# An encoder's attention, by pairs of heads and halves of the queries

## The chip, the cores and the metric

One core of a Trainium2 chip runs the whole kernel as one program. The metric is the device time of one execution in microseconds; lower is better. Engine names are those of the profile: PE is TensorE, PEld its weight loads, DVE VectorE, ACT ScalarE, POOL GpSimd, SP the queue that issues most DMAs.

## The reference

Two encoder layers over 1024 tokens of width 1024, in float32. The even layer mixes tokens by latent attention (8 heads, q and k of 96 features, v of 64) and by retention, the odd layer by gated linear attention; each ends in a gated MLP. The change touches the attention alone:

```python
q = _rmsnorm(q, q_head_norm); k = _rmsnorm(k, k_head_norm)      # then rotary on the last 32 features
def block(qi):
    s = jnp.einsum('bqhd,bkhd->bhqk', qi, k).astype(jnp.float32) * MLA_QK ** -0.5
    p = jax.nn.softmax(s, axis=-1).astype(v.dtype)
    return jnp.einsum('bhqk,bkhe->bqhe', p, v)
```

## The kernel before

Most products are made in float32 precision from two parts: an operand is cast to float32r on ACT (`hi`) and the rest is taken on DVE or POOL (`lo = x - hi`, `split`, L327 to L330). `mm3` (L348 to L354) then makes three matmuls, hi by hi, hi by lo and lo by hi. A matmul of two plain float32 operands does it in one call, which stands in the trace as two records.

The attention is written in class `Mla`. `produce(pr)` makes q, k and v of a pair of heads for all tokens (plain float32 matmuls, L1555 and L1557), with v split, and with 64 columns of ones beside v (zeros in the low part). `prepare(i)` transposes q and k of a head, splits them, and finds each query's largest score over keys with 16 matmuls of 128x512 (L1610), each reduced on DVE (L1611); the negated maximum becomes row 96 of q (L1619), against a row of ones in k, so that the score comes out shifted. `attend(i)` goes, for one head, over two halves of 512 queries and eight tiles of 128 keys: an `mm3` for the scores, Exp on ACT (L1639), a split of the result (ACT, then DVE or every second time POOL, L1640), and, four tiles later (`AHEAD`), `product` (L1649): an `mm3` with [v, ones], so that rows 64 to 127 of the output are the softmax's denominators. After the last key tile it copies numerator and denominator (L1657, L1658); after the second head of a pair it divides (Ln, Exp, a Newton step, L1664 to L1668) and sends the result to DRAM or, for the last pair's first half, splits it.

The work is emitted by generators that are woven: `even` (L643) runs, for each head i, `attend(i)` with 16 steps and beside it `prepare(i + 1)` (13 steps) and, for even i below 6, `produce` of the next pair (10 steps); with heads 6 and 7 it runs the first operands and weights of the output projection (`early`, `weights`). A scheduler in the tile framework can move instructions from that order where they are ready. PSUM has eight banks: five of one rotation (`mm`), three of the other (`mr`, for `prepare` and `produce`). SBUF tiles come from rotations by tag: `raw` 2, `w` 6, `hx` 32, `hf` 22, `hr` 16, `pg` 3 buffers.

Of the kernel before, what the change touches and what calls it, by code (L numbers as in the profile page):

```python
# [10 lines left out]
F32 = mybir.dt.float32  # L11
# [21 lines left out]
RG = 8, 17  # L33
SECOND = 5
AHEAD = 4
GLA_STEPS, GLA_TICKS = 38, (42, 34)
GATES = 6, 7, 0, 1, 2, 3, 4, 5
EARLY = 4
# [30 lines left out]
class Encoder:  # L69
# [573 lines left out]
    def even(self, h, win, ws):  # L643
# [44 lines left out]
        def many(*gens):  # L688
            for g in gens:
                yield from g  # L690
# [38 lines left out]
        def weights():  # L729
            first.append(self.out_weights(w, 0))  # L730
            yield
# [1 line left out]
        rest = many(mixed(proj_qk(3), norms()), rg(0, 1, 2, 3))  # L733
        self.weave(ret(2), 19, islice(rest, W2), W2)
        self.weave(ret(3), 19, rest, 39 - W2)
        for i in range(8):
            side, n = [], 0
            if i < 7:
                side.append(self.on((1, 1), m.prepare(i + 1)))
                n += 13  # L740
            if i % 2 == 0 and i < 6:
                side.append(self.on((0, 1), m.produce(i // 2 + 1)))
                n += 10
            if i >= 6:
                side.append(self.on((1, 0), many(early(0, 4, 5, 6, 7, 0, 1)) if i == 6 else
                                    many(early(0, 2), weights(), early(1, 4, 5, 6, 7, 0, 1, 2))))
                n += 6 if i == 6 else 9
            self.weave(m.attend(i), 2 * NT - 2 * (i < 6), many(*side), n)
        outs = [(o_a[p], None) for p in range(4)] + [(o_r[p], gates[p]) for p in range(4)]
        return outs, *o, w, [], first[0]  # L750

# [771 lines left out]
class Mla:  # L1523


    def __init__(self, e, outs, parts):
        self.e, self.nc, self.outs, self.parts = e, e.nc, outs, parts
        self.wq = e.io["mla_w_uq"][0].rearrange("(k p) f -> p k f", p=P)
        self.wkv = e.io["mla_w_ukv"][0].rearrange("(k p) f -> p k f", p=P)
        self.pair, self.head, self.behind = {}, {}, []  # L1530

    def produce(self, pr):

        e, nc = self.e, self.nc
        krr, krs = e.kr
        w1, w2 = (e.page(s, F32, "w") for s in ([P, 3, 192], [P, 2, 256]))
        nc.sync.dma_start(out=w1, in_=self.wq[:, :, blk(pr, 192)])
        nc.sync.dma_start(out=w2, in_=self.wkv[:, :, blk(pr, 256)])
        qp, kp, vp = [], [], []
        self.pair[pr] = qp, kp, vp  # L1540
        heads = lambda ap, f: ap.rearrange("p (n f) -> p n f", f=f)
        c2, s2 = e.rot[0]
        for hf in range(2):
            st, y, z = (e.small([P, 4, 4]) for _ in range(3))
            for t in range(4 * hf, 4 * hf + 4):
                c = t % 2
                if not c:
                    qp.append(e.page([P, 2, 192], tag="hx"))
                    kp.append(e.page([P, 2, 192], tag="hx"))
                    vp.append([e.page([P, 2, 2, P], F32R, tag="hx") for _ in range(2)])  # L1550
                    for v, x in zip(vp[-1], (1.0, 0.0)):
                        nc.gpsimd.memset(v[:, :, :, 64:].bitcast(F32), x)
                ps = e.bank()
                for k in range(3):
                    nc.tensor.matmul(ps[:, :192], lhsT=e.cq[k][hf][:, blk(t % 4)], rhs=w1[:, k], start=k == 0, stop=k == 2)  # L1555
                for k in range(2):
                    nc.tensor.matmul(ps[:, 256:], lhsT=e.ckv[k][hf][:, blk(t % 4)], rhs=w2[:, k], start=k == 0, stop=k == 1)  # L1557
                pk = heads(ps[:, 256:], 128)
                for j in range(2):
                    junk = e.half([P, P])  # L1560
                    nc.scalar.activation(junk[:, :96], ps[:, blk(j, 96)], AF.Square, accum_out=st[:, t % 4, j:j + 1])
                    nc.scalar.activation(junk[:, :64], pk[:, j, :64], AF.Square, accum_out=st[:, t % 4, 2 + j:3 + j])
                e.split(pk[:, :, 64:], *(v[:, c, :, :64] for v in vp[-1]))
                nc.vector.tensor_copy(qp[-1][:, c], ps[:, :192])
                nc.vector.tensor_copy(heads(kp[-1][:, c], 96)[:, :, :64], pk[:, :, :64])
                yield
            nc.vector.tensor_tensor(st[:, :, 2:], st[:, :, 2:], krs[:, blk(hf, 4)].unsqueeze(2).broadcast_to([P, 4, 2]), ALU.add)
            nc.vector.tensor_scalar(st, st, 1.0 / 96, EPS, ALU.mult, ALU.add)
            e.rsqrt(st, y, z)
            for i in range(2 * hf, 2 * hf + 2):  # L1570
                ts = blk(i, 2)
                q4, k4 = (x[i].rearrange("p c (n f) -> p c n f", f=96) for x in (qp, kp))
                yv = lambda o, w: y[:, blk(i % 2, 2), o:o + 2].unsqueeze(3).broadcast_to([P, 2, 2, w])
                tb = lambda v, w: v[:, ts, w].unsqueeze(2).broadcast_to([P, 2, 2, w.stop - w.start])
                nc.vector.tensor_tensor(q4, q4, yv(0, 96), ALU.mult)
                nc.vector.tensor_tensor(k4[:, :, :, :64], k4[:, :, :, :64], yv(2, 64), ALU.mult)
                nc.vector.tensor_tensor(k4[:, :, :, 64:], tb(krr, slice(0, 32)), yv(2, 32), ALU.mult)
                r = q4[:, :, :, 64:]
                a, b = e.half([P, 2, 2, 32]), e.half([P, 2, 2, 32])
                nc.vector.tensor_tensor(a, r, tb(c2, slice(0, 32)), ALU.mult)  # L1580
                for j in range(2):
                    nc.vector.tensor_tensor(b[:, :, :, blk(j, 16)], r[:, :, :, blk(1 - j, 16)], tb(s2, blk(j, 16)), ALU.mult)
                nc.vector.tensor_tensor(r, a, b, ALU.add)
            yield

    def prepare(self, i):
# [1 line left out]
        e, nc = self.e, self.nc  # L1588
        qp, kp, _ = self.pair[i // 2]
        hc = blk(i % 2, 96)  # L1590
        qs, ks = e.new_split(1), e.new_split(1)
        for t in qs.hi[0] + qs.lo[0] + ks.hi[0] + ks.lo[0]:
            nc.gpsimd.memset(t[96:].bitcast(F32), 0.0)
        for hf in range(2):
# [25 lines left out]
        self.head[i] = qs, ks  # L1620
        yield

    def attend(self, i):

        e, nc = self.e, self.nc
        qs, ks = self.head.pop(i)
        for hf in range(2):
            q, pa = qs.half(0, hf), e.bank()
            for kt in range(NT):
                if i > 5:  # L1630
                    x = e.page([P, H2], tag="hf")
                else:
                    if kt % 2 == 0:
                        two = e.page([P, 2, H2], tag="raw")
                    x = two[:, kt % 2]
                ps = e.bank()
                both = e.page([P, 2, H2], F32R, "w")
                e.mm3(ps, ks.tok(0, kt), q, True, True)
                nc.scalar.activation(x, ps, AF.Exp, scale=96 ** -0.5)  # L1639
                e.split(x, both[:, 0], both[:, 1], nc.gpsimd if kt % 2 and i < 7 else None)  # L1640
                self.behind.append((i, hf, kt, pa, both))
                if len(self.behind) > AHEAD:
                    self.product(*self.behind.pop(0))
                yield
        while self.behind and i == 7:
            self.product(*self.behind.pop(0))
            yield

    def product(self, i, hf, kt, pa, both):  # L1649
        e, nc = self.e, self.nc  # L1650
        pr, rows, cs = i // 2, blk(i % 2, 64), halves()[hf]
        e.mm3(pa, [v[:, kt % 2, i % 2] for v in self.pair[pr][2][kt // 2]], (both[:, 0], both[:, 1]), kt == 0, kt == NT - 1)
        if kt < NT - 1:
            return
        if i % 2 == 0 and not hf:
            self.o, self.den = (e.page([P, S]) for _ in range(2))
        nc.scalar.copy(self.o[rows, cs], pa[:64])  # L1657
        nc.vector.tensor_copy(self.den[rows, cs], pa[64:])  # L1658
        if i % 2:

            if not hf:
                self.y, self.outs[pr] = e.page([P, S]), e.waiting()
            o, z, y = self.o[:, cs], self.den[:, cs], self.y[:, cs]
            nc.scalar.activation(y, z, AF.Ln)  # L1664
            nc.scalar.activation(y, y, AF.Exp, scale=-1.0)
            nc.vector.scalar_tensor_tensor(z, z, -1.0, y, ALU.mult, ALU.mult)
            nc.vector.scalar_tensor_tensor(y, z, 2.0, y, ALU.add, ALU.mult)
            nc.vector.tensor_tensor(o, o, y, ALU.mult)  # L1668
            if pr == 3 and not hf:
                self.parts[pr] = hi, lo = [e.page([P, H2], F32R, "hx") for _ in range(2)]  # L1670
                e.split(o, hi, lo)
            else:
                nc.sync.dma_start(out=self.outs[pr][hf], in_=o)


def encoder(tc, io):
# [39 lines left out]
```

## Time and profile before

| | |
|---|---|
| median of 3 runs | 2552.49 us (2551.14 to 2555.01) |
| profiled execution, its time | 2551.83 us |
| profiled execution, its span | 2549.8 us |
| TensorE's granted clock, mean | 0.995 |
| PE busy | 2496.8 us (98%) |
| DVE, ACT, POOL busy | 71%, 47%, 11% |

The span reaches from the first to the last instruction; the time has 2.0 us more around it. A busy PE counts a matmul from its start to its modelled end, while the next one has already started, so that a stretch can be 98% busy without being full; the distance between starts tells more.

### The profile page before, as it was taken

Reading aid. Unit: us, or ns where it says so; the run is one execution under the profiler, and the core shown is the slowest. Engines: PE = TensorE matmul, PEld = TensorE weight load, DVE = VectorE, ACT = ScalarE, POOL = GpSimd, SP = SyncE. Lnnn points to the kernel's source line nnn. Section 1 sums busy time; section 2 is a strip of 40 time slices with the busy share of each in tenths; the row PEclk is TensorE's granted clock in tenths of the full one; section 3 lists DMA queues with packets and bytes.
Section 4 is the critical chain, followed back from the end, with each engine's and each line's share of the span. In section 5 each row is a group of like instructions: output and inputs, shape, how many; then the busy total and the mean of one; then the engine's idle time right before and its main releaser. Section 6 shows DMA issues by size and latency. Waiting matters only on the chain.

```text
span 2549.8 us, 33347 instructions
## 1 busy us (share of the span) xinstructions
PE 2496.8 (98%) x12584; PEld 2091.4 (82%) x12584; DVE 1800.3 (71%) x2855; ACT 1209.2 (47%) x2229; POOL 269.8 (11%) x286
## 2 busy tenths in 40 slices
PE   8999989999999999999999999999999999999999
PEld 8989877777888888887788898897788888887787
DVE  6545887878578877778767545648578777778762
ACT  5333767778444333334434445657444333334432
POOL 0000033443000000003240000000000000004240
PEclk9999999999999999999999999999999999999999
DMA  6111100003632333437524211223822332437523
GB/s 196 40 46 42 51 26 5 14 18 124 202 95 87 103 109 98 130 97 259 162 68 149 60 55 42 73 69 108 260 83 95 105 111 87 132 102 253 165 69 122
DMA packets 305814, 262.21 MB, mean 103 GB/s; under 512 B 15916, under 2 KB 240277, under 8 KB 305653
## 3 DMA queue, kind: packets, MB, share of 16 engines
q1 hardware_dynamic: 301045, 251.69, 31.2%
q10 hardware_dynamic: 4608, 8.39, 0.9%
q8 instruction: 99, 1.62, 0.3%
q14 instruction: 62, 0.51, 0.1%
HBM read 189.52 MB, written 70.52 MB: 102 GB/s over the span
## 4 chain that ended last, share of the span: by engine, by line
PE 68%; DVE 17%; ACT 6%; DMA 6%; issue 3%; POOL 1%; SPq 0%; DVEq 0%; ACTq 0%; POOLq 0%
PE mm L351 58%; DMA raw<-in_ffn_w_up 3%; DVE pg L1291 2%; ACT w L329 2%; DVE w L330 1%; DVE hx L1261 1%; PE mr L1104 1%; PE mr L351 1%; PE mr L1555 1%; DVE pg L1295 1%; PE mr L1557 1%; DVE hx L330 1%; DVE sr L1611 1%; DVE wf L330 1%; PE mr L854 1%
## 5 line engine op out<-in xcount | busy, mean ns | idle before, releaser
L351 PE MATMUL mm<-hx,w 128*128 128x512 f32 (+1 forms) x3408 | 831.1, 394 | 6.9 <-ACT h L329 4.9
L351 PEld LDWEIGHTS mm<-hx,w 128*128 128x128 f32 (+1 forms) x3408 | 636.3, 188 | 144.8 <-ACT w L329 5.7
L351 PE MATMUL mm<-h,w 128*128 128x512 f32 x1800 | 433.6, 394 | 7.5 <-ACT w L329 4.9
L329 ACT CAST w<-raw 128x1024 fp32r<-128x1024 f32 (+3 forms) x307 | 245.1, 802 | 347.2 <-PE mm L351 211.8
L351 PEld LDWEIGHTS mm<-h,w 128*128 128x128 f32 x1800 | 339.8, 190 | 80.5 <-ACT w L329 5.8
L330 DVE TENSOR_TENSOR w<-raw,w 128x1024 fp32r<-128x1024 f32 (+3 forms) x257 | 254.5, 993 | 177.1 <-ACT w L329 161.2
L351 PE MATMUL mm<-w,hx 128*128 128x256 f32 (+1 forms) x2304 | 363.9, 305 | 2.8 <-POOL w L330 2.3
L351 PE MATMUL mm<-h,wf 128*128 128x512 f32 x1368 | 329.2, 389 | 1.4 <-DVE wf L330 0.8
L351 PEld LDWEIGHTS mm<-w,hx 128*128 128x128 f32 x2304 | 307.4, 191 | 21.9 <-POOL w L330 3.3
L351 PEld LDWEIGHTS mm<-h,wf 128*128 128x128 f32 x1368 | 256.5, 188 | 56.3 <-DVE wf L330 1.7
L1397 POOL TENSOR_TENSOR hx<-raw 128x512 f32<-128x512 f32 (+1 forms) x10 | 12.6, 1260 | 1535.4 <-DMA raw<-in_ffn_w_down 1008.1
L329 ACT CAST wf<-raw 128x1024 fp32r<-128x1024 f32 x78 | 82.1, 1052 | 182.7 <-DVE raw L1247 134.5
L1261 DVE TENSOR_TENSOR hx<-mm,hx 128x512 f32<-128x512 f32 x190 | 130.1, 685 | 45.9 <-PE mm L351 45.9
L351 PE MATMUL mm<-hx,wf 128*128 128x512 f32 x552 | 132.1, 389 | 0.0
L351 PEld LDWEIGHTS mm<-hx,wf 128*128 128x128 f32 x552 | 103.5, 188 | 21.9 <-DVE hx L1261 0.4
L330 DVE TENSOR_TENSOR wf<-raw,wf 128x1024 fp32r<-128x1024 f32 x78 | 95.5, 1224 | 18.9 <-ACT wf L329 18.9
L351 PE MATMUL mm<-hr,hr 128*128 128x512 f32 x336 | 104.2, 404 | 1.3 <-ACT hf L1639 1.3
L1292 ACT ACTIVATE pg<-pg 128x1024 f32<-128x1024 f32 x44 | 46.7, 1062 | 121.9 <-DVE pg L1291 121.8
L1291 DVE SCALAR_TENSOR_TENSOR pg<-mm,c,pg 128x512 f32<-128x512 f32 (+1 forms) x100 | 73.7, 747 | 30.0 <-ACT pg L1286 30.0
L351 PE MATMUL mm<-hf,w 128*128 128x512 f32 x384 | 88.8, 392 | 0.0
L351 PEld LDWEIGHTS mm<-hf,w 128*128 128x128 f32 x384 | 72.2, 188 | 16.0
L330 POOL TENSOR_TENSOR w<-raw,w 128x512 fp32r<-128x512 f32 (+1 forms) x50 | 68.5, 1369 | 138.9 <-ACT w L329 96.9
(385 smaller groups left out, 3384.2 us busy)
## 6 DMA issues: line engine op xcount, KB each, us to landing
raw<-in_ffn_w_up SPq DMA_DIRECT2D x88, 512.0 KB
pg<-d SPq DMA_DIRECT2D x52, 512.0 KB
d<-tt SPq DMA_DIRECT2D x64, 256.0 KB
d<-pg SPq DMA_DIRECT2D x55, 256.0 KB
raw<-in_ffn_w_down SPq DMA_DIRECT2D x32, 384.0 KB
raw<-in_w_in_odd SPq DMA_DIRECT2D x24, 512.0 KB
raw<-in_w_out_even SPq DMA_DIRECT2D x16, 512.0 KB
rb<-in_ffn_w_down SPq DMA_DIRECT2D x32, 256.0 KB
```

Of the source, the lines that this page charges most:

```text
L329: self.nc.scalar.copy(hi, src)
L330: return (rest or self.nc.vector).tensor_tensor(lo, src, hi.bitcast(F32), ALU.subtract)
L351: mm = lambda w, x, start, stop: self.nc.tensor.matmul(out, lhsT=w, rhs=x, start=start, stop=stop, skip_group_check=more)
L854: self.nc.tensor.transpose(ps[:, blk(j)], src[:, j], self.ident)
L1104: nc.tensor.matmul(ps, lhsT=w[:, blk(t % 4)], rhs=x, start=n == 0, stop=n == len(terms) - 1)
L1261: add = lambda out, x, y: nc.vector.tensor_tensor(out, x, y, ALU.add)
L1291: nc.vector.scalar_tensor_tensor(dst, g[hf][:, src], cw(tap), dst, ALU.mult, ALU.add)
L1292: nc.scalar.activation(cv, cv, AF.Silu)
L1295: nc.vector.tensor_tensor(cv[:, sl], cv[:, sl], v[hf], ALU.mult)
L1555: nc.tensor.matmul(ps[:, :192], lhsT=e.cq[k][hf][:, blk(t % 4)], rhs=w1[:, k], start=k == 0, stop=k == 2)
L1557: nc.tensor.matmul(ps[:, 256:], lhsT=e.ckv[k][hf][:, blk(t % 4)], rhs=w2[:, k], start=k == 0, stop=k == 1)
L1611: nc.vector.tensor_reduce(mx[:, 2 * t + hf:2 * t + hf + 1], ps, AX.X, ALU.max)
```

## The change

Attention goes by pairs of heads. For each half of the queries the first head's eight key tiles are scored and exponentiated, all eight results being kept, then the second head's. The weights are not split any more: both heads' products with v are plain float32 matmuls with 64 columns of weights, the one head's into PSUM rows 0 to 63 and the other's into rows 64 to 127 of the same bank, two key tiles (four calls) at a time. The ones beside v are gone: GpSimd adds the eight exponentiated tiles of each head (seven adds of 128x512), and two plain float32 matmuls of ones with these sums make the denominators of both heads. The division follows a step later. v is not split. The generators beside it are one list, dealt out at `PACE`: 13/8 items a step for the first eight steps, then 9/8.

```diff
+PACE = 13 / 8, 9 / 8
...
-        for i in range(8):
-            side, n = [], 0
...
-            self.weave(m.attend(i), 2 * NT - 2 * (i < 6), many(*side), n)
+        order = [("p", 1)] + [x for p in range(1, 4) for x in (("k", p), ("p", 2 * p), ("p", 2 * p + 1))]
+        side = many(*(self.on((0, 1), m.produce(x)) if kind == "k" else self.on((1, 1), m.prepare(x)) for kind, x in order),
+                    self.on((1, 0), many(early(0, 4, 5, 6, 7, 0, 1, 2), early(1, 4, 5, 6, 7, 0, 1, 2), weights())))
+        done = 0
+        for i, _ in enumerate(many(*(m.attend(p) for p in range(4))), 1):
+            while done < PACE[0] * min(i, 8) + PACE[1] * max(i - 8, 0):
+                done += 1
+                next(side, None)
...
-        w1, w2 = (e.page(s, F32, "w") for s in ([P, 3, 192], [P, 2, 256]))
-        nc.sync.dma_start(out=w1, in_=self.wq[:, :, blk(pr, 192)])
+        w1, w2 = [e.page([P, 192], tag="hx") for _ in range(3)], e.page([P, 2, 256], tag="hx")
+        for k in range(3):
+            nc.sync.dma_start(out=w1[k], in_=self.wq[:, k, blk(pr, 192)])
...
-                    vp.append([e.page([P, 2, 2, P], F32R, tag="hx") for _ in range(2)])
-                    for v, x in zip(vp[-1], (1.0, 0.0)):
-                        nc.gpsimd.memset(v[:, :, :, 64:].bitcast(F32), x)
+                if t % 4 == 0:
+                    vp.append(e.page([P, 4, 2, 64], tag="hx"))
...
-                e.split(pk[:, :, 64:], *(v[:, c, :, :64] for v in vp[-1]))
+                nc.scalar.copy(vp[-1][:, t % 4], pk[:, :, 64:])
...
-        qs, ks = e.new_split(1), e.new_split(1)
+        qs, ks = (e.new_split(1, "hx" if i % 2 else None) for _ in range(2))
...
+    def attend(self, pr):
         e, nc = self.e, self.nc
         for hf in range(2):
+            acc, xs = e.page([P, 2, H2]), [[], []]
+            for j in range(2):
+                qs, ks = self.head[2 * pr + j]
+                for kt in range(NT):
+                    if j and pr == 3:
+                        x = e.page([P, H2], tag="hf")
+                    else:
+                        if kt % 2 == 0:
+                            two = e.page([P, 2, H2], tag="raw" if j else "w")
+                        x = two[:, kt % 2]
+                    xs[j].append(x)
+                    ps = e.bank()
+                    e.mm3(ps, ks.tok(0, kt), qs.half(0, hf), True, True)
+                    nc.scalar.activation(x, ps, AF.Exp, scale=96 ** -0.5)
+                    if kt:
+                        nc.gpsimd.tensor_tensor(acc[:, j], acc[:, j] if kt > 1 else xs[j][0], x, ALU.add)
+                    if j:
+                        self.behind.append((pr, hf, kt, xs[0][kt], x, acc))
+                    if self.behind and (kt % 2 if j else True) and len(self.behind) > (AHEAD - 1) * j:
+                        self.products()
+                    elif self.later and not j:
+                        self.later.pop(0)()
+                    yield
...
+    def products(self):
...
+        for pr, hf, kt, *xs, acc in [self.behind.pop(0) for _ in range(2)]:
+            if not kt:
+                self.pa = e.bank()
+            v = self.pair[pr][2][kt // 4]
+            for j in range(2):
+                nc.tensor.matmul(self.pa[blk(j, 64)], lhsT=v[:, kt % 4, j], rhs=xs[j], start=kt == 0, stop=kt == NT - 1)
+        if kt == NT - 1:
+            oy = e.page([P, 2, H2])
+            nc.scalar.copy(oy[:, 0], self.pa)
+            self.later.append(lambda: self.divide(pr, hf, acc, oy[:, 0], oy[:, 1]))
+
+    def divide(self, pr, hf, acc, o, y):
...
+        z, ps = e.half(), e.bank()
+        for j in range(2):
+            nc.tensor.matmul(ps[blk(j, 64)], lhsT=e.ones[:, :64].bitcast(F32), rhs=acc[:, j], start=True, stop=True)
+        nc.scalar.activation(y, ps, AF.Ln)
+        nc.scalar.activation(y, y, AF.Exp, scale=-1.0)
+        nc.vector.scalar_tensor_tensor(z, ps, -1.0, y, ALU.mult, ALU.mult)
+        nc.vector.scalar_tensor_tensor(y, z, 2.0, y, ALU.add, ALU.mult)
+        nc.vector.tensor_tensor(o, o, y, ALU.mult)
```

## Rows read from the trace of the kernel before

**Rows 1.** The page: span, and busy us (share) xinstructions of each engine.

```profile
span 2549.8 us, 33347 instructions
...
PE 2496.8 (98%) x12584; PEld 2091.4 (82%) x12584; DVE 1800.3 (71%) x2855; ACT 1209.2 (47%) x2229; POOL 269.8 (11%) x286
```

**Rows 2.** Busy time in stretches: the attention, then heads 2 and 3.

```profile
core 0: us, PE busy (x) PEld busy (x) DVE busy (x) ACT busy (x) POOL busy (x), PEclk, DMA share, GB/s
366.00:651.00 285.00, 273.83 (x1300) 222.59 (x1299) 234.43 (x464) 228.42 (x583) 109.66 (x138) 0.99 0.15 46
...
441.00:484.00 43.00, 42.27 (x213) 35.90 (x211) 32.17 (x76) 33.91 (x117) 15.63 (x24) 1.00 0.09 26
484.00:516.00 32.00, 29.94 (x142) 23.39 (x141) 28.56 (x53) 25.03 (x47) 16.50 (x20) 1.00 0.00 1
```

**Rows 3.** Groups by form, 366 to 651 us: busy us, mean ns | idle before.

```profile
L351 PE MATMUL mm<-w,hx 128*128 128x512 f32 x384 | 117.9, 399 | 0.5 <-POOL w L330 0.4
L351 PE MATMUL mm<-hr,hr 128*128 128x512 f32 x336 | 104.2, 404 | 1.3 <-ACT hf L1639 1.3
...
L1611 DVE TENSOR_REDUCE sr<-mr 128x1 f32<-128x512 f32 x112 | 71.3, 680 | 1.9 <-PE mr L1610 1.6
L330 POOL TENSOR_TENSOR w<-raw,w 128x512 fp32r<-128x512 f32 x48 | 63.7, 1327 | 124.5 <-ACT w L329 82.4 <-issue 14.4 <-PE mm L351 12.9
...
L329 ACT CAST w<-raw 128x512 fp32r<-128x512 f32 x96 | 59.5, 625 | 5.4 <-PE mm L351 3.1
L1639 ACT ACTIVATE raw<-mm 128x512 f32<-128x512 f32 x96 | 57.2, 604 | 26.5 <-PE mm L351 21.7 <-POOL w L330 2.0 <-issue 1.2
L1610 PE MATMUL mr<-hr,hr 128*128 128x512 f32 x112 | 43.3, 402 | 1.9 <-DVE sr L1611 1.8
L330 DVE TENSOR_TENSOR w<-raw,w 128x512 fp32r<-128x512 f32 x48 | 36.9, 769 | 11.4 <-ACT w L329 11.4
L1555 PE MATMUL mr<-w,hf 128*128 128x192 f32 x144 | 27.5, 327 | 0.0
L1557 PE MATMUL mr<-w,hf 128*128 128x256 f32 x96 | 24.6, 379 | 0.0
...
L1593 POOL MEMSET hr<- 32x512 f32 x48 | 23.4, 522 | 7.8 <-POOL w L330 2.6 <-issue 2.4 <-PE mm L351 1.9
...
L351 PE MATMUL mm<-hf,hf 128*128 128x512 f32 x48 | 14.6, 397 | 0.8 <-ACT hf L1619 0.8
```

**Rows 4.** PE in order of time: start us, us from first start to last end.

```profile
410.05 0.86 PE L351 MATMUL mm<-w,hx 128*128 128x512 f32 x3
410.75 0.86 PE L351 MATMUL mm<-hr,hr 128*128 128x512 f32 x3
```

**Rows 5.** The same view, two tokens' tiles of plain float32 matmuls in `produce`.

```profile
403.61 1.14 PE L1555 MATMUL mr<-w,hf 128*128 128x192 f32 x6
...
404.58 1.03 PE L1557 MATMUL mr<-w,hf 128*128 128x256 f32 x4
```

**Rows 6.** The same view, retention's matmuls with 64 weight columns, both heads.

```profile
196.03 0.52 PE L351 MATMUL mm<-w,hx 128*128 128x256 f32 x3
196.47 0.44 PE L835 MATMUL mr<-hr,hf 128*64 128x128 f32 x4
...
198.12 0.41 PE L837 MATMUL mr<-hr,hr 128*64 128x128 f32 x4
198.46 0.51 PE L351 MATMUL mm<-w,hx 128*128 128x256 f32 x2
```

**Rows 7.** PE's waits, 366 to 651 us: total, times, longest.

```profile
PE mr L1598 <- DVE hx L1583: 6.5, 3, 2.7
```

**Rows 8.** Busy time in stretches of 2 us about head 1's start.

```profile
414.00:416.00 2.00, 0.00 (x0) 0.00 (x0) 2.00 (x5) 1.15 (x3) 1.09 (x1) 0.96 0.00 0
416.00:418.00 2.00, 1.87 (x8) 1.65 (x9) 2.00 (x8) 0.00 (x0) 0.00 (x0) 0.50 0.00 0
```

More of the change, by code (lines that the diff above doesn't have):

```diff
@@ L735, in even @@
         self.weave(ret(3), 19, rest, 39 - W2)
-        for i in range(8):
-            side, n = [], 0
[L738 to L747, printed above, removed]
-            self.weave(m.attend(i), 2 * NT - 2 * (i < 6), many(*side), n)
+        order = [("p", 1)] + [x for p in range(1, 4) for x in (("k", p), ("p", 2 * p), ("p", 2 * p + 1))]
[6 more added lines that the diff above has]
+                next(side, None)
+        for _ in side:
+            pass
         outs = [(o_a[p], None) for p in range(4)] + [(o_r[p], gates[p]) for p in range(4)]
@@ L1529, in __init__ @@
         self.wkv = e.io["mla_w_ukv"][0].rearrange("(k p) f -> p k f", p=P)
-        self.pair, self.head, self.behind = {}, {}, []
+        self.pair, self.head, self.behind, self.later = {}, {}, [], []
     def produce(self, pr):
@@ L1549, in produce @@
                     kp.append(e.page([P, 2, 192], tag="hx"))
-                    vp.append([e.page([P, 2, 2, P], F32R, tag="hx") for _ in range(2)])
-                    for v, x in zip(vp[-1], (1.0, 0.0)):
-                        nc.gpsimd.memset(v[:, :, :, 64:].bitcast(F32), x)
+                if t % 4 == 0:
+                    vp.append(e.page([P, 4, 2, 64], tag="hx"))
                 ps = e.bank()
                 for k in range(3):
-                    nc.tensor.matmul(ps[:, :192], lhsT=e.cq[k][hf][:, blk(t % 4)], rhs=w1[:, k], start=k == 0, stop=k == 2)
+                    nc.tensor.matmul(ps[:, :192], lhsT=e.cq[k][hf][:, blk(t % 4)], rhs=w1[k], start=k == 0, stop=k == 2)
                 for k in range(2):
@@ L1621, in prepare @@
         yield
-    def attend(self, i):
+    def attend(self, pr):
         e, nc = self.e, self.nc
-        qs, ks = self.head.pop(i)
         for hf in range(2):
[L1628 to L1646, printed above, removed]
+            acc, xs = e.page([P, 2, H2]), [[], []]
[21 more added lines that the diff above has]
+                    yield
+        del self.head[2 * pr], self.head[2 * pr + 1]
+        while pr == 3 and self.behind:
+            self.products()
@@ L1647, in attend @@
             yield
-    def product(self, i, hf, kt, pa, both):
+        if pr == 3:
+            self.later.pop(0)()
+            yield
+    def products(self):
         e, nc = self.e, self.nc
[L1651 to L1673, printed above, removed]
@@ new lines, in divide @@
+    def divide(self, pr, hf, acc, o, y):
+        e, nc = self.e, self.nc
+        z, ps = e.half(), e.bank()
[6 more added lines that the diff above has]
+        nc.vector.tensor_tensor(o, o, y, ALU.mult)
+        if not hf:
+            self.outs[pr] = e.waiting()
+        if pr == 3 and not hf:
+            self.parts[pr] = hi, lo = [e.page([P, H2], F32R, "hx") for _ in range(2)]
+            e.split(o, hi, lo)
+        else:
+            nc.sync.dma_start(out=self.outs[pr][hf], in_=o)
```

## The prediction

> **What bounds the kernel now.** I read the page first: PE is busy nearly all the time and the other engines are not [rows 1], so an edit is worth what it takes from PE's own stream or from PE's waits. Busy says little here, because a matmul of 512 columns stands with 399 ns [rows 3] while three of them start within 0.70 us of each other, 0.233 us apart [rows 4]. So I count the attention by distances. In its 285 us [rows 2] PE has 384 records of products with v, 384 of scores and 112 for the maxima [rows 3]: 880 x 0.233 = 205.0 us. `produce` adds 144 records of 192 columns and 96 of 256 [rows 3]. Their distances follow from [rows 5]: (1.14 - 0.327) / 5 = 0.163 us and (1.03 - 0.379) / 3 = 0.217 us, together 44.3 us. Both are 0.85 ns a column. The other 1300 - 880 - 240 = 180 records [rows 2] are mostly of 128 columns, 0.109 us each, 19.6 us. That makes 269 us of stream and **16 us of idle PE**. Head 2, which has `produce` beside it, is full: 112 x 0.233 + 48 x 0.163 + 32 x 0.217 + 21 x 0.109 = 43.2 of its 43 us. Head 3, without, has 29.4 of 32. The idle is where DVE is late: the chain into the transposes [rows 7], once a stretch with PE empty and DVE full, after which the granted clock was 0.50, the 1.2 GHz level [rows 8].
>
> **The change part by part.**
>
> *Products with v.* Removed: 384 x 0.233 = 89.5 us. Added: 32 blocks of four plain float32 calls. A call is two records; at 0.85 ns a column one of 512 columns takes 0.434 us, so a block in series is 8 x 0.434 = 3.47 us, and more than the 12 x 0.233 = 2.80 us that it replaces. All hangs on whether the two heads' calls, with 64 weight columns each and different PSUM rows, run side by side. No attention row shows it; retention has the same arrangement at 128 columns [rows 6]: 32 records that would take 3.47 us in series are over 1.99 us after the first start, when the next full matmul starts. That is half of the series, 1.74 us, and 0.25 us for entering, leaving and imperfect pairing. I take it over: 1.74 + 0.25 = 1.99 us a block, 63.7 us in all. Bounds: 55.7 us (nothing lost at the ends) and 119 us (series, with the same 0.25).
>
> *Denominators.* Eight times two calls of ones: 0.87 + 0.25 = 1.12 us, 9.0 us (7.0 to 15.9). Before they came free with the products. So PE's stream changes by 63.7 + 9.0 - 89.5 = **-16.8 us**, between -26.8 and +45.4.
>
> The Trainium skill has a rule against this: "TensorEngine Tiling (Array Packing)", section Key Properties, says that going from one tiling mode to another drains the engine. The trace agrees that the ends cost something, but 0.25 us for both ends together, less than one matmul's length; a full drain at each end is priced among the rivals.
>
> *Splits of the weights.* ACT's 128 casts of 0.63 us (96 of them in one group, 59.5 us [rows 3]) go, and DVE's and POOL's subtractions with them. DVE's 72 at 0.7 to 0.77 us take some 53 us. These are not PE's work; they were cover for nothing, and where DVE was late they help. ACT keeps the Exp of 0.60 us a step.
>
> *GpSimd's sums.* 112 adds. The nearest row is its subtraction of the same size, 1.327 us [rows 3]: 149 us instead of 75, with some 30 us of memsets [rows 3], 179 of 270 us. It stays hidden behind PE. Queued behind an add are the next adds and `prepare`'s memsets, for which its matmuls wait; the two `raw` buffers wait for adds too, but four tiles later. Below the row I see no reason for less than 1.2 us, above it 1.4; neither matters until an add takes (270 - 30) / 112 = 2.1 us.
>
> *v unsplit, weights of `produce` in other buffers, three DMAs for one on SP.* Nothing on PE. SP has some 50 issues in the whole attention, so two more a pair are covered; without that cover, two issues of about 0.4 us at a time when the weights are needed nine steps later.
>
> *The order.* This moves idle, not work. A step of the first head (scores only) now has 0.70 us of PE besides the side work, a step of the second head 0.70 + 1.0. The maxima are where DVE is slower: an item is two matmuls, 0.47 us, and two reductions, 1.36 us [rows 3]. By the items dealt out, a pair's eight steps of maxima for its second head fall just on the first head's steps of the next stretch, and `prepare` ends in the very step before its use. Then:
> - pair 0, first eight steps (all 13 items): PE 5.6 + 3.7 + 2.3 = 11.6; DVE 16 x 0.68 and four splits of 0.7 = 13.7 and some 2 us of end chain (reduction, ACT's copy of the row): 4 us idle;
> - pairs 1 to 3, first eight: PE 1.99 + 1.12 + 5.6 + 3.7 + 0.5 = 12.9; DVE 10.9 + 2.1 for the division, and the same 2 us of chain: 2 us each, 6;
> - second half's first eight with the end of `produce`: the chain into the transposes, up to 2.7 us a time [rows 7], three times: 8;
> - the last pair's second half: ACT 8 x 0.60 + 8 x 0.62 + 1.2 = 11 against PE 1.99 + 1.12 + 5.6 = 8.7: 2.3.
>
> Together 20.4 us against 15.8 today: **+4.6 us**. Low bound 0 (the scheduler fills the holes; then -15.8), high bound twice the sum (+25), since chains can add up.
>
> **Sum.** 2551.8 (the profiled execution, 0.7 below the median shown) - 16.8 + 4.6 = 2539.6, about **2540 us**, 12 us or 0.5% less.
>
> **The rivals.**
> 1. *The holes are filled.* Heads 0, 2 and 4 run full today although DVE works there too, and with 53 us less DVE the 2 us chains may hide. Idle no more than 6 and ends at 0.1: 2551.8 - 22 - 10 = 2520. Against it: a first-head step has little PE work to draw on.
> 2. *A block slips by a record*, since a call's second record must wait for its first: +0.434 x 40 = 17.4, 2557: no change to speak of. [Rows 6] show pairs of four records throughout, which speaks against it.
> 3. *Full drain.* If each end of 40 blocks empties the array for a matmul's 0.399 us, the ends take 32 us and not 10: 2562. The rows bear out little of it. This is the rule of "TensorEngine Tiling (Array Packing)" taken at its word.
> 4. *Slower: the light stretches starve PE.* Eight stretches of first-head steps, each 3 us worse than above: a stall of 1.7 and then a clock at 0.50 as in [rows 8], which loses 1.3. 2539.6 + 24 = 2564. It decides from 12.2 / 8 = 1.5 us a stretch on. For it: DVE, POOL (9.3 of adds and 5 of memsets in eight steps) and PE are all within a few us of each other there.
> 5. *Not side by side at 512 columns*: two streams of 512 float32 columns might not be fed at once. +45.4 for -16.8: 2602. Only the width speaks for it.
>
> **How the numbers follow.** Forecast (2530 to 2547) 0.50; rival 1 (2518 to 2530) 0.18; rival 2 0.11; rival 3 0.05; rival 4 0.10; rival 5 0.05; the rest 0.01. Less than 0.2%, 5.1 us, can't be told from no change here. Faster: the first two, 0.68. Same: most of rival 2 and small shares of the forecast's neighbours, 0.12. Slower: 0.20. The range 2522 to 2558 holds the forecast, most of rival 1 and rival 2, some 0.78 to 0.8.
>
> **What would show it.** Right: records of 128x512 with 64 weight columns, eight in about 1.9 us from the block's start to the next full matmul; PE's stream in the attention some 17 us shorter; DVE busy about 165 us there and POOL about 180; PE's waits, if any, on the reductions, the row copy and `produce`'s chain. Wrong: such a block over 2.4 us (rivals 2, 3, 5); PE waiting for POOL's adds or memsets; stretches of clock at 0.50 in the first head's steps (rival 4); or an attention as long as before with a shorter stream, which would mean that the idle grew by as much.

## The result and the profile after

The changed kernel takes 2583.5 us (median of 4 runs, 2583.2 to 2584.9) against 2551.8 us before: 1.0126 times, with an interval of 1.0108 to 1.0144. It is 31.7 us slower, and 43.5 us above the forecast. TensorE has less to do and needs longer. The page of the changed kernel, its span, busy times and granted clock in 40 slices, against [rows 1]:

```profile
span 2581.4 us, 32905 instructions
...
PE 2514.8 (97%) x12488; PEld 2044.0 (79%) x12488; DVE 1758.9 (68%) x2735; ACT 1135.0 (44%) x2093; POOL 339.2 (13%) x310
...
PEclk9999999998999999999999999999999999999999
```

DVE and ACT lost work, POOL gained 69 us of it, and PE is busy for 18 us more with 96 instructions fewer. From PE's first score to the first sum of the output projection on DVE it is 321.9 us, before 286.6: the attention is 35 us longer, and the rest of the kernel is not. The same view of stretches as [rows 2], of the attention and then of 8 us in it:

```profile
365.00:686.00 321.00, 295.30 (x1207) 176.15 (x1207) 192.58 (x355) 154.05 (x448) 180.76 (x169) 0.94 0.15 49
...
418.00:420.00 2.00, 0.16 (x1) 0.00 (x0) 2.00 (x3) 0.56 (x1) 1.92 (x2) 1.00 0.00 0
420.00:422.00 2.00, 0.00 (x0) 0.00 (x0) 2.00 (x3) 0.00 (x0) 1.79 (x2) 1.00 0.00 0
422.00:424.00 2.00, 1.93 (x9) 1.58 (x10) 2.00 (x9) 0.58 (x1) 0.00 (x0) 0.63 0.00 0
424.00:426.00 2.00, 2.00 (x7) 1.53 (x6) 1.62 (x3) 1.16 (x3) 1.10 (x1) 0.51 0.00 0
```

Two things are read from the first row. PE stands without work for 321.0 - 295.3 = 25.7 us, before 11.2. And its granted clock is 0.94 where it was 0.99: 321 x 0.06 = 19 us lost at half speed, before 1.7 us, in a single spell [rows 8]. The four rows below show one such event: 4 us in which PE has nothing while DVE is full, then the 1.2 GHz level. Of the seven spells at that level, together 37 us, this is one. Who is waited for, in PE's waits of the changed kernel, 366 to 680 us (total, times, longest), against [rows 7]:

```profile
PE mr L1597 <- DVE hx L1582: 8.7, 4, 3.9
...
PE mr L1617 <- DVE sr L1612: 7.3, 4, 2.3
...
PE mm L352 <- ACT w L1640: 3.2, 1, 3.2
```

These are the ends of two chains: `produce`'s k into its transposes (L1597), and the last reduction of `prepare` into the transposed maximum (L1617). A third loss shows in no list of waits, since PE counts as busy to a matmul's end. The maxima's matmuls in PE's order of time, in the first eight steps of pair 0 and of pair 1:

```profile
373.32 6.59 PE L1609 MATMUL mr<-hx,hx 128*128 128x512 f32 x12
...
460.53 2.88 PE L1609 MATMUL mr<-hx,hx 128*128 128x512 f32 x5 [0.28 <-DVE sr L1610]
```

Where the next one waits for a reduction they start 0.60 us apart, the pace of DVE's reductions, and not 0.233: 22 times in the changed kernel, 8 us in all, and never in the kernel before. The 3.9 us stop, in order of time for DVE, POOL and PE (start, us to the last end, in brackets the wait before):

```profile
417.61 4.25 POOL L1642 TENSOR_TENSOR pg<-pg,w 128x512 f32<-128x512 f32 x3 [1.10 <-ACT w L1640]
417.79 1.42 DVE L1581 TENSOR_TENSOR hf<-hx,c 128x64 f32<-128x64 f32 x2
...
419.14 1.61 DVE L1574 TENSOR_TENSOR hx<-hx,sm 128x384 f32<-128x384 f32 x1
...
420.68 1.34 DVE L1582 TENSOR_TENSOR hx<-hf,hf 128x128 f32<-128x128 f32 x1
...
422.07 1.20 PE L1597 MATMUL mr<-c,hx 128*96 128x128 f32 x6 [3.91 <-DVE hx L1582]
...
423.56 0.27 DVE L1582 TENSOR_TENSOR hx<-hf,hf 128x128 f32<-128x128 f32 x1
```

POOL makes three adds in a row, from 417.61 to 421.86. In just that time DVE's small operation L1582 takes 1.34 us; the next one of the same line, after POOL has stopped, takes 0.27. The groups by form of the changed kernel, 366 to 680 us, where [rows 3] stood before:

```profile
L1610 DVE TENSOR_REDUCE sr<-mr 128x1 f32<-128x512 f32 x112 | 70.9, 680 | 16.5 <-PE mr L1609 16.5
L1642 POOL TENSOR_TENSOR pg<-pg,w 128x512 f32<-128x512 f32 x48 | 68.7, 1432 | 20.1 <-ACT w L1640 17.1
...
L1666 PE MATMUL mm<-w,hx 128*64 128x512 f32 x128 | 64.7, 618 | 0.0
L1666 PE MATMUL mm<-raw,hx 128*64 128x512 f32 x96 | 47.8, 608 | 0.0
...
L1574 DVE TENSOR_TENSOR hx<-hx,sm 128x384 f32<-128x384 f32 x12 | 8.8, 730 | 0.2
...
L1582 DVE TENSOR_TENSOR hx<-hf,hf 128x128 f32<-128x128 f32 x12 | 6.0, 502 | 0.1
```

The add itself is near the forecast (1.43 us, 1.33 forecast). The reductions, which read PSUM, take 680 ns as before. The operations with two SBUF inputs do not. Last, the products, in PE's order of time: a block of four calls up to the next full matmul, and then part of a block that the scheduler has split.

```profile
411.04 0.64 PE L1666 MATMUL mm<-w,hx 128*64 128x512 f32 x1
411.05 0.64 PE L1666 MATMUL mm<-raw,hx 128*64 128x512 f32 x1
...
412.91 0.64 PE L1597 MATMUL mr<-c,hx 128*96 128x128 f32 x4
...
430.49 1.07 PE L1666 MATMUL mm<-w,hx 128*64 128x512 f32 x2
431.49 0.73 PE L1609 MATMUL mr<-hr,hr 128*128 128x512 f32 x2
```

The two heads' records start 0.01 us apart, and the whole block takes 412.91 - 411.04 = 1.87 us: they do run side by side. A call that stands alone holds PE for 1.00 us; in a whole block the four calls take 0.47 us each.

### The profile page after: what moved, and what is told of

Read it like the earlier page. It is cut to its first block, busy times and chain, and to the rows that moved or that the text cites. A ratio compares the mean times of both kernels' runs of the same rounds, so it can differ in the third digit from the quotient of the medians.

```text
span 2581.4 us, 32905 instructions
## 1 busy us (share of the span) xinstructions
PE 2514.8 (97%) x12488; PEld 2044.0 (79%) x12488; DVE 1758.9 (68%) x2735; ACT 1135.0 (44%) x2093; POOL 339.2 (13%) x310
## 4 chain that ended last, share of the span: by engine, by line
PE 66%; DVE 5%; DMA 3%; ACT 2%; issue 1%; POOL 1%; SPq 0%; POOLq 0%; DVEq 0%; ACTq 0%
PE mm L352 59%; PE mr L1103 1%; PE mr L352 1%; PE mm L1666 1%; DMA pg<-d 1%; PE mr L1033 1%; DVE hx L331 1%; PE mr L1078 1%; POOL pg L1642 1%; DMA raw<-in_ffn_w_down 0%; DVE w L331 0%; DMA raw<-in_w_out_odd 0%; DVE xa L1154 0%; DVE h L331 0%; ACT w L330 0%
## 5 line engine op out<-in xcount | busy, mean ns | idle before, releaser
L330 ACT CAST w<-raw 128x1024 fp32r<-128x1024 f32 (+3 forms) x211 | 185.8, 883 | 334.5 <-PE mm L352 219.5
L331 DVE TENSOR_TENSOR w<-raw,w 128x1024 fp32r<-128x1024 f32 (+3 forms) x209 | 221.1, 1061 | 163.4 <-ACT w L330 137.2
L352 PE MATMUL mm<-w,hx 128*128 128x256 f32 x1920 | 246.1, 286 | 2.3 <-POOL w L331 1.8
L352 PEld LDWEIGHTS mm<-w,hx 128*128 128x128 f32 x1920 | 235.6, 192 | 4.8 <-POOL w L331 2.4
L1610 DVE TENSOR_REDUCE sr<-mr 128x1 f32<-128x512 f32 x112 | 70.9, 680 | 16.5 <-PE mr L1609 16.5
L1642 POOL TENSOR_TENSOR pg<-pg,w 128x512 f32<-128x512 f32 x48 | 68.7, 1432 | 20.1 <-ACT w L1640 17.1
```

The source lines that it names most:

```text
L330: self.nc.scalar.copy(hi, src)
L331: return (rest or self.nc.vector).tensor_tensor(lo, src, hi.bitcast(F32), ALU.subtract)
L352: mm = lambda w, x, start, stop: self.nc.tensor.matmul(out, lhsT=w, rhs=x, start=start, stop=stop, skip_group_check=more)
L1610: nc.vector.tensor_reduce(mx[:, 2 * t + hf:2 * t + hf + 1], ps, AX.X, ALU.max)
L1642: nc.gpsimd.tensor_tensor(acc[:, j], acc[:, j] if kt > 1 else xs[j][0], x, ALU.add)
```

## The experiments

Three theories stood at the start. The first: stretches of scores alone give PE too little, so that a chain on DVE that ends late stops it, and the half clock follows (rival 4). The second: the adds on GpSimd hold up DVE's operations with two SBUF inputs, and so the same chains. The third: the products themselves are dearer than 1.99 us a block. Medians are in us; ratios are to the kernel before, run beside each.

**Slack for the chains.** Only the pace of the side work changes, so that `prepare` and `produce` end some steps ahead of their use.

```diff
-PACE = 13 / 8, 9 / 8
+PACE = 16 / 8, 9 / 8
```

> The changed kernel with PACE = 16/8, 9/8: the work beside the attention runs three items further ahead, so that a head's preparation ends two to three steps before its scores are wanted and not in the step before. Theory 1 (the order starves PE: the maxima, bound by DVE, and the chain at the end of each preparation fall on steps with nothing but scores, and the clock drops after each stop): the four stops of 2.0 to 2.8 us at the chain's end and about half of the 37 us of half clock go, 2583 - 9 - 9 = 2565, between 2558 and 2575. Theory 2 (GpSimd's sums hold the others up): no change, 2580 to 2586. Theory 3 (the float32 products themselves are dearer than reckoned): no change.

2558.2, ratio 1.0028 (1.0016 to 1.0040): 25.3 of the 31.7 us back, from the order alone. Its PE waits, 366 us to the end of the attention:

```profile
PE mr L1617 <- DVE sr L1612: 7.0, 4, 3.0
PE mm L1677 <- POOL pg L1642: 3.1, 1, 3.1
...
PE mr L1597 <- DVE hx L1582: 1.9, 2, 0.9
```

The transposes no longer wait for long (8.7 us before the edit, 1.9 now), though L1582 is as slow as it was (496 ns). The waits at the end of `prepare` (L1617) are as long as before (7.3 us), where the first theory had them go; but the clock falls less behind them: 14 us at the lower level in the attention instead of 37. One wait has grown, from 0.6 to 3.1 us: the last division, for the sums.

**No sums.** The adds are left out, and a constant row stands in for them: the sum over keys is left out of the denominators.

```diff
-                    if kt:
-                        nc.gpsimd.tensor_tensor(acc[:, j], acc[:, j] if kt > 1 else xs[j][0], x, ALU.add)
...
-            nc.tensor.matmul(..., rhs=acc[:, j], start=True, stop=True)
+            nc.tensor.matmul(..., rhs=e.row[:, :H2], start=True, stop=True)
```

> The changed kernel without GpSimd's 112 adds; the denominators are made from a constant row, so the sums over keys are left out. Theory 1: little, within 6 us of 2583. Theory 2: most of the 44 us between forecast and measurement goes, 2545 to 2560. Theory 3: no change.

2558.9, ratio 1.0026 (1.0016 to 1.0036): 24.6 us back with the tight order kept. So the sums, costed at nothing, are worth as much as the order. The attention in the view of stretches, and the largest of its PE waits:

```profile
366.00:664.00 298.00, 287.43 (x1214) 175.33 (x1213) 161.59 (x356) 154.22 (x448) 22.02 (x46) 0.96 0.17 54
...
PE mr L1617 <- DVE sr L1612: 6.9, 4, 2.0
```

The transposes (L1597) don't wait for L1582 at all any more: in this order that wait needs the adds. The four waits at the end of `prepare` stay, each comes with a spell at the 1.2 GHz level, and at 0.96 the clock loses 298 x 0.04 = 12 us. That is the order's own cost, without the sums.

**Both: slack and no sums.** The two edits above together, the sums again left out.

> The changed kernel with both the slack (PACE 16/8) and the sums left out. Slack alone and no sums alone each took 25 us. If they act on different stops the gains add, 2533 to 2540. If each merely uncovers the same stops (a chain that is late because DVE was slowed is hidden by slack as well), most of the second 25 us is already taken: 2545 to 2556.

2536.2, ratio 0.9945 (0.9926 to 0.9965): 47.3 us below the changed kernel, and 3.8 below the forecast. The two gains nearly add (25.3 + 24.6 = 49.9). The attention in this kernel, in the view of stretches, and the two groups of DVE:

```profile
366.00:641.00 275.00, 269.12 (x1208) 168.56 (x1207) 161.26 (x355) 156.23 (x448) 22.07 (x46) 0.99 0.18 58
...
L1574 DVE TENSOR_TENSOR hx<-hx,sm 128x384 f32<-128x384 f32 x12 | 6.7, 555 | 0.2
...
L1582 DVE TENSOR_TENSOR hx<-hf,hf 128x128 f32<-128x128 f32 x12 | 3.4, 285 | 0.1
```

PE is without work for 5.9 us, the clock is back at 0.99, and L1582 takes 285 ns instead of 502. As many instructions of DVE, 355, take 161.3 us here and 192.6 in the changed kernel: with the adds DVE loses 31 us, all on operations with two SBUF inputs. The products kept their form here, so the third theory can have no more than the few us by which their stream was mis-sized.

**Sums on DVE**, with the slack:

```diff
-                        nc.gpsimd.tensor_tensor(acc[:, j], ...
+                        nc.vector.tensor_tensor(acc[:, j], ...
```

> The changed kernel with slack and the 112 adds on DVE. GpSimd then slows nobody, but DVE has 112 x 0.7 = 78 us more. Theory 1: the steps with scores alone and maxima have DVE 5 us further over PE in each of eight stretches, so slower than with slack alone, 2570 to 2600. Theory 2: DVE's slowing (some 15 us in all) goes and the 78 us are mostly hidden, 2550 to 2560.

2571.7, ratio 1.0085 (1.0064 to 1.0105): 13.5 us above the same order with the adds on GpSimd. An add takes 0.68 us there, but the 112 of them, 77 us, stand in the queue of the engine that PE waits for. The second theory's 2550 to 2560 is missed: the 77 us are not hidden. GpSimd is the better of two dear places.

**Sums made, not read**, with the slack: the adds run, and the constant row is used for the denominators.

```diff
-            nc.tensor.matmul(..., rhs=acc[:, j], start=True, stop=True)
+            nc.tensor.matmul(..., rhs=e.row[:, :H2], start=True, stop=True)
```

> Slack (PACE 16/8), and GpSimd makes all its adds, but the denominators come from a constant row, so that nobody reads the sums; the sum over keys is left out of the result. With the adds made and used it was 2558, without them 2536. If the cost is that the division waits for the last add, and what stands behind that: 2536 to 2543. If it is that an add under way holds up DVE's operations with two SBUF inputs: unchanged, 2553 to 2561.

2554.2, ratio 1.0008 (0.9998 to 1.0019): 4.0 us less than with the sums read. The wait of the division is about that (3.1 us above). 18 us above the kernel without adds remain, though nobody reads the sums.

**One input instead of two**, with the slack and the constant row: GpSimd writes as much and reads half, and the sums are left out.

```diff
-                        nc.gpsimd.tensor_tensor(acc[:, j], acc[:, j] if kt > 1 else xs[j][0], x, ALU.add)
+                        nc.gpsimd.tensor_scalar(acc[:, j], x, 1.0, None, ALU.mult)
```

> Slack, and in place of each of GpSimd's adds a multiplication of one tile by 1.0: as many operations of 128x512, with one SBUF input; the sums over keys are left out. If any busy GpSimd holds DVE up, DVE's late operations stay in proportion to GpSimd's time, 2548 to 2558. If it takes two inputs, 2536 to 2543 and no DVE operation of two inputs over 0.75 us.

2542.5, ratio 0.9961 (0.9945 to 0.9976): 11.6 us less than the adds that nobody reads, in intervals that don't meet. Groups of this kernel, 366 us to the end of the attention:

```profile
L1642 POOL TENSOR_SCALAR pg<-w 128x512 f32<-128x512 f32 x56 | 83.9, 1498 | 44.5 <-ACT w L1640 29.3 <-PE mr L1609 11.9
...
L1582 DVE TENSOR_TENSOR hx<-hf,hf 128x128 f32<-128x128 f32 x12 | 4.6, 386 | 0.1
```

GpSimd is occupied for longer, 1.50 us an operation, and DVE is held up less (386 ns; 496 with the adds). One input still holds it up somewhat: an operation of 128x256 (L1575) takes up to 0.83 us, not the 0.75 expected at most, against 1.51 beside the adds and 0.42 alone. Exp's longest wait for a `raw` buffer that GpSimd still reads is no shorter than with the adds (6.1 us, 5.0), so the buffers are not the difference. So it is not GpSimd's own queue that costs, but what the second input takes from DVE.

**Adds in halves**, with the slack: each add as two of 256 columns.

```diff
+                        for c in (blk(0, 256), blk(1, 256)):
-                        nc.gpsimd.tensor_tensor(acc[:, j], ...
+                            nc.gpsimd.tensor_tensor(acc[:, j, c], ...
```

> Slack, with each add of 512 columns as two of 256, the same sums. If DVE's operation waits for the end of the add under way, its waits are half as long, some 0.65 us and not 1.3, and the chain into the transposes with it: 2546 to 2554, though GpSimd's work grows by its fixed cost an instruction. If what counts is GpSimd's total time: 2558 to 2566.

2556.8, ratio 1.0021 (1.0011 to 1.0032), which can't be told from the slack alone (1.0016 to 1.0040): a miss. The group of its adds:

```profile
L1643 POOL TENSOR_TENSOR pg<-pg,w 128x256 f32<-128x256 f32 x96 | 74.9, 814 | 10.7 <-ACT w L1640 10.2
```

The longest operation of DVE on 128x128 beside such an add is 0.82 us, against 1.37 beside a whole one, so the single delay follows the add's length. The time did not. Twice 0.81 us is more than 1.43, and GpSimd is busy for 206 us in the attention instead of 183. The trace shows where that goes, in PE's largest waits:

```profile
PE mm L1678 <- POOL pg L1643: 6.2, 2, 4.8
PE mr L1617 <- DVE sr L1612: 5.1, 4, 1.5
```

The waits for DVE are shorter than with whole adds (5.1 us at the end of `prepare` instead of 7.0, none for L1582 instead of 1.9), and the division waits for the sums longer, 6.2 us instead of 3.1. So this run does not tell what the delays cost: it traded one wait for another. Which of the delays make up the 11.6 us is open.

**Products one after the other.** Both heads' calls go to PSUM rows 0 to 63 of the same bank; the second head's result is mixed into the first's, and the result is copied twice.

```diff
-                nc.tensor.matmul(self.pa[blk(j, 64)], lhsT=..., rhs=xs[j], start=kt == 0, stop=kt == NT - 1)
+                nc.tensor.matmul(self.pa[:64], lhsT=..., rhs=xs[j], start=kt == 0 and not j, stop=kt == NT - 1 and j == 1)
```

> The changed kernel with both heads' products into the same PSUM rows 0 to 63, which takes away their running side by side (the sum of two heads' results stands in both, so the output is not the attention's). All theories: if the two calls ran side by side, a block of 1.99 us becomes 3.5 to 3.7, 32 x 1.6 = 51 us more stream, less the stops that it covers: 2610 to 2635. If they did not, 2583.

2609.6, ratio 1.0233 (1.0213 to 1.0254), 26 us above the changed kernel, just under the lower edge of what was expected. A block in PE's order of time:

```profile
394.72 1.07 PE L1666 MATMUL mm<-w,hx 128*64 128x512 f32 x2
395.63 1.02 PE L1666 MATMUL mm<-raw,hx 128*64 128x512 f32 x2
396.49 1.02 PE L1666 MATMUL mm<-w,hx 128*64 128x512 f32 x2
397.35 1.02 PE L1666 MATMUL mm<-raw,hx 128*64 128x512 f32 x2
398.30 0.96 PE L352 MATMUL mm<-hx,hx 128*128 128x512 f32 x3
```

398.30 - 394.72 = 3.58 us against 1.87: side by side is worth 1.71 us a block, 55 us over 32 blocks. Only 26 us show in the time. Where the rest went, in the view of stretches:

```profile
366.00:713.00 347.00, 331.63 (x1207) 186.79 (x1207) 185.91 (x355) 158.77 (x455) 178.26 (x169) 0.97 0.14 46
```

PE without work is 15.4 us instead of 25.7, and at 0.97 the clock loses 347 x 0.03 = 10 us instead of 19 (12 by the spells themselves): a longer stream covers 17 to 19 us of the stops and of what follows them. The other 10 or so were never there: split blocks gain less by running side by side, and from start to start the products grew by 44 us, not 55.

**Counter-phase.** `prepare(1)` goes ahead of the attention and the side work is dealt out so that `produce`, which is PE's work, runs beside scores alone and `prepare`, which is DVE's, beside the products: of a pair's 32 steps the first eight take 10 items of `produce`, and steps 8 to 16 and 24 to 32 take 13 of `prepare` each.

```diff
-        order = [("p", 1)] + [x for p in range(1, 4) ...]
+        order = [x for p in range(1, 4) ...]
...
-            while done < PACE[0] * min(i, 8) + PACE[1] * max(i - 8, 0):
+            while done < due(i):
...
-        ... many(m.produce(0), m.prepare(0)) ...
+        ... many(m.produce(0), m.prepare(0), m.prepare(1)) ...
```

> The changed kernel with the side work in counter-phase: both heads of the first pair are prepared before the attention, then each pair's first eight steps (scores only) carry the next pair's projections, which are PE's own work, and the steps with products carry the maxima. Every stretch but the scores of a pair's second half then has PE as the engine with most work (23 us against DVE 20, 17 against 14). Theory 1: 35 to 45 us less than the changed kernel, 2538 to 2550, and little half clock left in the attention. Theories 2 and 3: the same sums and products, so at least 2570.

2604.7, ratio 1.0206 (1.0189 to 1.0223): 21 us above the changed kernel where the first theory expected a gain. Its PE waits, the largest of the attention:

```profile
PE mr L1606 <- DVE hx L1591: 13.6, 3, 5.1
...
PE mm L1686 <- POOL pg L1651: 5.1, 2, 3.0
PE mr L1606 <- DVE hx L335: 4.8, 1, 4.8
PE mr L1563 <- ACT hf L1569: 4.5, 1, 4.5
```

The attention also starts later, at 390 us instead of 366, since `prepare(1)` stands ahead of it; that alone is more than the 21 us. What the first theory speaks of is gone: no wait at the end of `prepare`, and the maxima stand 0.60 us apart once instead of 22 times. But the chains that feed the transposes again end just ahead of their use, and the stops there are longer (5.1 against 3.9 us). The run moved the stops, and decides nothing on the first theory.

**Scores of both heads in turn.** One key tile of the first head, one of the second, so that no stretch but the very first is without products; the exponentiated tiles then share the `w` buffers; side work with three steps of slack (13 items by step 6.5, then 36 for each pair, done by steps 30, 61 and 93).

```diff
-            for j in range(2):
...
-                for kt in range(NT):
+            for j, kt in ... [(j, kt) for kt in range(NT) for j in range(2)]:
...
-            while done < PACE[0] * min(i, 8) + PACE[1] * max(i - 8, 0):
+            while done < due(i):
```

> The changed kernel with the scores of both heads of a pair taken by turns, key tile by key tile (all but the very first half of the queries), so that products with v stand in every fourth step and no stretch has scores alone; each head is prepared three steps ahead. The same products and the same sums on GpSimd. Theory 1 (PE starves where scores stand alone beside DVE-bound work without slack): the attention falls to its stream of some 255 us and 10 to 20 us of idle, 2530 to 2550, under the kernel before. Theory 2 (GpSimd's adds slow DVE's operations with two SBUF inputs, and with them the chain from the projections to the transposes, wherever they stand): the adds are as many, so 2550 to 2560 as with the slack alone.

2574.2, ratio 1.0093 (1.0077 to 1.0110): 9 us better than the changed kernel, 16 worse than the slack alone, and outside what either theory gave (2530 to 2550, 2550 to 2560). Its PE waits, 366 to 680 us:

```profile
PE mr L1602 <- DVE hx L1587: 11.4, 5, 3.5
...
PE mr L1559 <- DVE hx L1569: 4.4, 2, 2.3
PE mm L1684 <- POOL pg L1649: 3.3, 4, 2.0
```

The same chain into the transposes waits, here almost without stretches of scores alone. Why it waits more than with the slack is not shown.

**The old order with unsplit weights.** The kernel before, with plain float32 weights and one call of 128 columns, [v, ones], a head; no sums, no pairs.

```diff
-                    vp.append([e.page([P, 2, 2, P], F32R, tag="hx") for _ in range(2)])
+                    vp.append(e.page([P, 2, 2, P], tag="hx"))
...
-        e.mm3(pa, [v[:, kt % 2, i % 2] for v in ...], (both[:, 0], both[:, 1]), kt == 0, kt == NT - 1)
+        nc.tensor.matmul(pa, lhsT=...[:, kt % 2, i % 2], rhs=x, start=kt == 0, stop=kt == NT - 1)
```

> The kernel before, in its own order by heads, with one part of the change: weights and v unsplit, each product one plain float32 call with [v, ones] over all 128 columns, no sums on GpSimd. A call is two records of 0.434 us in place of three of 0.233: 128 x (0.868 - 0.700) = 21.5 us more stream. Theory 1: the old order keeps PE fed, idle 16 us or less, so 2562 to 2575 and no more than one or two spells of half clock. Theory 3 (float32 products stall in themselves): over 2580. Theory 2 says nothing beyond theory 1 here.

2557.6, ratio 1.0022 (1.0012 to 1.0032), better than expected. The stream gains 128 x 0.868 - 89.5 = 21.6 us and the time only 5.8, so the 16 us of idle PE of the kernel before were gone: the splits had made them. They went from ACT, DVE and GpSimd together, so what each had done to PE is not shown apart.

**A version that beats both.** The kernel before with Exp writing float32r, and two matmuls, by the high and the low part of [v, ones]. The low part of the weights is left out, in numerator and denominator alike.

```diff
-                        two = e.page([P, 2, H2], tag="raw")
+                        two = e.page([P, 2, H2], F32R, "w")
...
-                e.split(x, both[:, 0], both[:, 1], nc.gpsimd if kt % 2 and i < 7 else None)
...
-        e.mm3(pa, [v[:, kt % 2, i % 2] for v in ...], (both[:, 0], both[:, 1]), kt == 0, kt == NT - 1)
+        for n, v in enumerate(self.pair[pr][2][kt // 2]):
+            nc.tensor.matmul(pa, lhsT=v[:, kt % 2, i % 2], rhs=x, start=kt == 0 and not n, stop=kt == NT - 1 and n == 1)
```

> The kernel before in its order by heads with the weights unsplit in another way: Exp writes them rounded to float32r, and they are multiplied with [v high, ones] and [v low, zeros], two matmuls of 0.233 us in place of three, numerator and denominator from the same rounded weights; the low part of the weights is left out. Stream 128 x 0.233 = 29.8 us less; DVE, ACT and GpSimd lose the splits; the idle of 16 us shrinks as it did with unsplit float32 weights in this order, where the attention had no stop over 1 us. 2551 - 30 - (0 to 14): 2507 to 2522 by every theory; over 2530 if projections, maxima and transposes then stop PE as they do in the changed kernel.

2509.6, ratio 0.9842 (0.9825 to 0.9859): 41 us below the kernel before and 74 below the changed one. Its attention in the view of stretches:

```profile
366.00:613.00 247.00, 243.96 (x1176) 199.67 (x1175) 181.03 (x397) 158.10 (x457) 33.02 (x78) 0.99 0.16 53
```

128 matmuls fewer are 128 x 0.233 = 29.8 us, and 11.2 - 3.0 = 8.2 us of PE without work are gone: 38 of the 41 us.

## Why the prediction was wrong

**The step that failed** is GpSimd's sums: "It stays hidden behind PE", "neither matters until an add takes (270 - 30) / 112 = 2.1 us". The adds were about of the size forecast (1.3 to 1.4 us) and hidden in GpSimd's own queue, and yet they cost 24.6 us in the changed order and 2558.2 - 2536.2 = 22.0 with the slack. The cover that I named was GpSimd's time; what they took was DVE's: 192.6 us of it in the attention, where the forecast had 165 and the kernel without adds has 161.3. Beside an add, L1582 takes up to 1.35 us, alone 0.28. With the slack, the 22.0 divide as the experiments stand: 6.3 for a one-input operation on GpSimd, 11.6 more for the second input, 4.0 for waiting on the sums themselves (the first and the last are small: their pairs of intervals overlap). That the second input does it is shown by the kernel with one input; by which of the delayed operations the 11.6 us come about is not, since halving the delays lengthened the wait for the sums by 3 us and gave nothing that can be measured.

The Trainium skill has the rule, in "GPSIMD Engine Reference", section "8. Key points": GpSimd shares its SBUF interfaces with VectorE, and contends with VectorE's instructions that have two SBUF inputs. The trace agrees: 502 ns beside the adds against 285 without for an operation with two SBUF inputs, 680 against 684 for the reductions from PSUM.

The trace of the kernel before had shown it already, beside GpSimd's subtractions. One group of DVE there, and the same operation in the kernel with slack and no sums:

```profile
L1576 DVE TENSOR_TENSOR hx<-hx,sm 128x256 f32<-128x256 f32 x12 | 8.3, 691 | 0.0
...
L1575 DVE TENSOR_TENSOR hx<-hx,sm 128x256 f32<-128x256 f32 x12 | 5.0, 419 | 0.0
```

The mean of 691 ns is made of nine at 0.42 us and three at 1.5 us, and the three are those that a subtraction ran beside.

**The second step that failed** is the order, the idle of 20.4 us for 15.8, "+4.6". The places were right: `produce`'s chain into the transposes, three times up to 2.7 us forecast, was waited for four times up to 3.9, and the end of `prepare` four times up to 2.3. The first of these waits belongs to the sums as much as to the order: either edit alone takes it away (1.9 us with the slack, none without the sums). What the order costs by itself is the end of `prepare` in the first head's steps. The waits there were forecast. What was missing is what goes with them: the maxima 0.60 us apart ahead of the stop, 8 us, and the half clock behind it, which the sum put at nothing although [rows 8] show it. PE without work grew by 25.7 - 11.2 = 14.5 us, and the half clock cost 19 us where it had cost 1.7. Ending the chains earlier gave 25.3 us back, so the price of the order is shown, and so is that it and the sums are two causes: together 47.3 us, the 43.5 of the miss and 3.8 more.

**The products** were nearly right. A block takes 1.87 us and some 0.10 for entering, against 1.99 forecast. Not forecast were the blocks that the scheduler splits, where a lone call takes 1.00 us: in the kernel with slack and no sums the 32 blocks come to some 69 us with their ends, about 5.5 over the 63.7, and the denominators to 9, as forecast. The -16.8 of the stream should have been about -11. In the changed kernel itself more blocks are split and they come to 75 us, the denominators to 11. With the 8 us of the maxima and some smaller losses that makes PE's stream there, counted from start to start without the waits that the view shows and at the full clock, 8 us longer than before and not 16.8 shorter. So the 35 us of the attention are 13 of waits, 14 of half clock outside of them, and 8 of stream.

**The splits of the weights**, said to help "where DVE was late", did: without them, the old order runs without its 16 us of idle. The new order, however, spent that on stops of its own.

**The rivals.** Rival 4, starved light stretches and then the half clock, is what the order does. Four of the seven spells at the lower level, 24 of 37 us, come with the stops of 1.5 to 2.3 us at the end of `prepare` in the first head's steps, where PE had run at the pace of DVE's reductions. It came in four stretches and not in eight, and with the sums left out the kernel takes 2558.9 us, near the 2564 that the rival gave. The other 24.6 us, of the sums, stood in no rival. Rival 5 is excluded by the block of 1.87 us against 3.58 in series, rival 3 by some 0.10 us at the entry. Rival 2 has no whole block that slips, only the split ones. Rival 1, holes filled, is near to what the kernel with slack and no sums shows, 5.9 us without work, with 5.5 us more of products.

## What to carry to other kernels

An engine with time to spare is no free place for work as long as it shares something with the engine that the bound waits for: look which operations of that engine run beside it, and what they take there and alone. Where work is dealt out over steps, let each chain end some steps ahead of its use; a stop of PE can be paid for twice, once itself and once in the clock behind it (19 us of clock for 25.7 without work in the changed kernel, but 3 for 18 with the adds in halves). A view of busy time does not show a PE that runs at another engine's pace: look at the distances between starts. A change that takes work from the bound engine is worth what its stream shrinks only if the stops don't grow, so price the chains first.

## What the runs showed of the hardware

GpSimd's multiplication with one SBUF input takes 1.50 us for 128x512 float32, no less than an add with two, 1.43; an add of 256 columns takes 0.81. Two float32 matmuls of 512 columns with 64 weight columns each and different PSUM rows run wholly side by side, 1.87 us for four calls against 3.58 in the same rows.
